# First norm's squares summed on TensorE, first layer's sine and cosine on GpSimd, two tiles of x on GpSimd's queue

## The chip, the cores and the metric

The kernel runs on one core of a Trainium2 chip. The metric is the device time of one launch in microseconds. The core has a matrix engine (TensorE, PE in the rows, its weight loads PEld), a vector engine (VectorE, DVE), a scalar engine (ScalarE, ACT), GpSimd (POOL) and a sync engine (SP) that here only issues transfers. Each engine works through its own list of instructions strictly in order, and an instruction that waits for another engine holds up everything behind it on its own engine.

## What is computed

Two transformer-like blocks over 512 tokens of width 1024, in f32. The change lies wholly within the start of the first layer of the first block:

```
h    = x * rsqrt(mean(x*x, axis=-1) + 1e-6) * norm_mix[0]
proj = h @ w_in[0]                 # q, k, v, conv inputs, u, gates
lam  = a_re + i*a_im;  dt = exp(log_dt)
lam_bar = exp(lam*dt) = exp(a_re*dt) * (cos(a_im*dt) + i*sin(a_im*dt))
b_bar   = (lam_bar - 1)/lam * b
states  = scan(lam_bar, u @ b_bar)    # the state-space branch, fed by u
```

After it come window attention, a short convolution, gates, a gated feed-forward part, a second such layer, then a block with two sparse attentions, an attention over a memory, and a feed-forward part.

## The kernel before

x lies transposed: eight tiles x0 to x7 of 128 features by 512 tokens, one f32 buffer each. A product is split for accuracy. `split` makes from a tile of x a rounded part (ScalarE, line 458) and a remainder (VectorE, line 462); `_split_` does the same with weights (lines 370 and 371). TensorE then does three matmuls for each pair of a 128x128 weight block and a tile: lines 438 to 440. The division by the norm is left until the products are evacuated: `RS` holds the inverse root, spread over all partitions.

Weights come in chunks of 512 KB, eight 128x128 blocks each, 24 matmuls for one chunk. There are three raw buffers, three rounded ones (`hi`) and three remainders (`lo`), used in turn, so chunk 6 needs the `hi` and `lo` of chunk 3 to be free. The first product, u, takes chunks 0 to 3: chunk 0 holds the blocks for x0 and x1, chunk 1 those for x2 and x3, and so on, four output tiles each, in four PSUM banks. Chunk 4 (the product k) reuses these banks, so it can't start before u is evacuated (line 580), which needs `RS`.

`RS` comes about as follows. `norm_add` (line 531) squares each tile on ScalarE and adds the squares into one tile `acc`, six of the seven additions on GpSimd (line 540). `norm_fin` sums `acc` over the partitions with 16 small matmuls against a column of ones (`tok_sums`, line 493 in `few`), takes the inverse root on VectorE (`rsqrt`, lines 482 to 488), and spreads it by four transposes (`nb`, line 504) and a copy on ScalarE (line 506).

Beside this `_ssm_tables` computes the tables of the state-space branch: a long run of tiny VectorE operations on 128x16 values (lines 837 to 849, 925 to 930): two exponentials, then `sincos`, then powers. `_gen_ssm` uses them.

The order of the instructions on each engine is made by a scheduler from priorities and its own estimates of durations. All transfers are issued by SP, in one order. A weight transfer waits in it until its raw buffer is free, and what stands behind it waits too.

Of the kernel before, what the change touches and what calls it, by code (L numbers as in the profile page):

```python
# [89 lines left out]
def _cst_layout():  # L90
    if _CST:
        return _CST
    o = 0
    for name, n in (("ident", 128), ("mask1", 256), ("maskc", 128), ("valid", 4), ("stack", 128),
                    ("ones2", 2), ("half2", 2), ("crope", 256)):
        _CST[name] = (o, n)
        o += n
    _CST["_n"] = (o, 0)
    return _CST
# [174 lines left out]
class _Net:  # L274
# [253 lines left out]
            self.nc.tensor.matmul(out[c:c + 64], pt[:, c:c + 64], v, start=start, stop=stop, skip_group_check=True)  # L528


    def norm_add(self, st, m, x, g, pool=False):
        nc = self.nc
        st["xg"][m] = self.split(x, g)
        if "acc" not in st:
            st["acc"] = self.slot()
            nc.scalar.activation(st["acc"], x, AF.Square)
        else:
            q = self.slot()
            nc.scalar.activation(q, x, AF.Square)
            (nc.gpsimd if pool else nc.vector).tensor_tensor(st["acc"], st["acc"], q, op=OP.add)  # L540
            self.rel(q)

    def norm_fin(self, st):

        st["rs"] = self.slot()
        yield
        ps = self.sb("nsum")
        self.tok_sums(lambda b: ps[:, b:b + 1], st["acc"])
        self.rel(st["acc"])
        r = self.small(4, tag="rs")  # L550
        self.rsqrt(r, ps[:, :4], 4, 1.0 / D, EPS)
        st["tok"] = r
        yield
        ps = self.sb("nb")
        self.bcast(lambda b: r[:, b:b + 1].to_broadcast([128, 128]), st["rs"], ps)
# [264 lines left out]
def _ssm_tables(N, i):  # L820

    nc = N.nc
    V = nc.vector
    W = 16
    n_tmp = [0]
    hold = [N.slot(), N.slot()]
# [7 lines left out]
    def ts(a, s1, s2=None, op0=OP.mult, op1=None, out=None, dt=FT):  # L834
        o = new(dt) if out is None else out
        if s2 is None:
            V.tensor_scalar(o, a, s1, None, op0=op0)
        else:
            V.tensor_scalar(o, a, s1, s2, op0=op0, op1=op1)
        return o  # L840

    def tt(a, b, op, out=None):
        o = new() if out is None else out
        V.tensor_tensor(o, a, b, op=op)
        return o

    def stt(a, s, b, op0, op1, out=None):
        o = new() if out is None else out
        V.scalar_tensor_tensor(o, a, s, b, op0=op0, op1=op1)
        return o  # L850

    def exp(x, out=None):
        x = ts(x, -87.0, 88.0, op0=OP.max, op1=OP.min)
        kf = ts(x, LOG2E, MAGIC, op0=OP.mult, op1=OP.add)
        ts(kf, MAGIC, op0=OP.subtract, out=kf)
        r = stt(kf, -0.693359375, x, OP.mult, OP.add)
        stt(kf, 2.12194440e-4, r, OP.mult, OP.add, out=r)
        p = ts(r, 1.0 / 5040.0)
        for k in (720.0, 120.0, 24.0, 6.0, 2.0, 1.0):
            stt(p, 1.0 / k, r, OP.add, OP.mult, out=p)  # L860
        ki = ts(kf, 127.0, op0=OP.add, dt=I32)
        k2 = ts(ki, 23, op0=OP.logical_shift_left, dt=I32)
        return stt(p, 1.0, k2.bitcast(FT), OP.add, OP.mult, out=out)
# [32 lines left out]
    lr, li = N.v(f"are{i}", 0, 16), N.v(f"aim{i}", 0, 16)  # L896
    dt = exp(N.v(f"ldt{i}", 0, 16))
    E = exp(tt(lr, dt, OP.mult))
    si, co = sincos(tt(li, dt, OP.mult))
    T = {}  # L900
    PWr = N.cp.tile([128, 16, 9], FT, tag="pwr", name="pwr")
    PWi = N.cp.tile([128, 16, 9], FT, tag="pwi", name="pwi")
# [81 lines left out]
    while n < 64:  # L984

        h = n // 2
        t1, t2 = t1s[:, :16].rearrange("p (a c) -> p a c", c=1), t2s[:, :16].rearrange("p (a c) -> p a c", c=1)
        hr, hi = Wr[:, :, h:h + 1], Wi[:, :, h:h + 1]
        cmul((Wr[:, :, n:n + 1], Wi[:, :, n:n + 1]), (hr, hi), (hr, hi), None, t1, t2)
        if n > 1:  # L990
            w1 = n - 1
            t1 = t1s[:, :16 * w1].rearrange("p (a c) -> p a c", a=16)
            t2 = t2s[:, :16 * w1].rearrange("p (a c) -> p a c", a=16)
            bb = lambda a: a[:, :, n:n + 1].to_broadcast([128, 16, w1])
            cmul((Wr[:, :, n + 1:2 * n], Wi[:, :, n + 1:2 * n]), (bb(Wr), bb(Wi)),
                 (Wr[:, :, 1:n], Wi[:, :, 1:n]), None, t1, t2)
        n *= 2
        yield
    N.rel(t1s, t2s, hold)
    T["w"] = (Wr, Wi)  # L1000
    N.ssm_t[i] = T
# [985 lines left out]
@with_exitstack  # L1987
def tile_two_blocks(ctx: ExitStack, tc: tile.TileContext, T, out, nch, parts=None, dump=None):
    nc = tc.nc
    N = _Net(ctx, tc, T, nch)  # L1990
    parts = parts or ("mix0", "ffn0", "mix1", "ffn1", "att2", "mem2", "mlp2")
    V, A = nc.vector, nc.scalar
    N.ssm_t = {}
    N.vec = N.keep([128, _vec_layout()["_n"][0]], FT, "vec")
    nk = _cst_layout()["_n"][0]
    N.cst = N.keep([128, -(-nk // 16) * 16], FT, "cst")[:, :nk]
    X = [N.slot() for _ in range(8)]
    nv = 64
    nc.sync.dma_start(N.vec[:, :nv], T["vec"][:, :nv])
    nc.sync.dma_start(X[0], T["xT"][0])  # L2000
    N.prefetch(1)
    for m in range(1, 8):
        nc.sync.dma_start(X[m], T["xT"][m])
        if m in (2, 5):
            N.prefetch(m)
        if m == 3:
            nc.sync.dma_start(N.vec[:, nv:], T["vec"][:, nv:])
    nc.sync.dma_start(N.cst, T["cst"])
    N.ident = N.c("ident")
    N.ones1 = N.c("ones2")[:, :1]  # L2010
    N.mask1 = N.keep([128, 256], BF, "mask1")

    wz = N.keep([128, 512], BF, "warm", "ssmc")
    nc.gpsimd.memset(wz, 0.0)
    ps = N.mm("warm")
    for _ in range(16):
        nc.tensor.matmul(ps, wz[:, :128], wz, start=True, stop=True)
    st = N.new_norm()

    def first(m):  # L2020
        nm = {"mix0": "norm_mix0", "ffn0": "norm_ffn0", "mix1": "norm_mix1", "ffn1": "norm_ffn1",
              "mem2": "norm2", "mlp2": "norm3"}.get(parts[0])
        if nm:
            N.norm_add(st, m, X[m], N.v(nm, m), pool=0 < m < 7)
        else:
            norm_add2(st, m, X[m], None)


    gg = N.keep([128, 16], FT, "gg")[:, :8]

    def norm_add2(st, m, x, _):
        st["xg"][m] = N.split(x, gg[:, m:m + 1])
        for key, g in (("acc", 1.0), ("acc2", N.v("norm_final", m))):
            if key not in st:
                st[key] = N.slot()
                A.activation(st[key], x, AF.Square, scale=g)
            else:
                q = N.slot()
                A.activation(q, x, AF.Square, scale=g)
                V.tensor_tensor(st[key], st[key], q, op=OP.add)  # L2040
                N.rel(q)

    for m in range(8):
        first(m)
        if m in (0, 2):
            N.presplit(m // 2 + 1)
    tab = None
    if parts[0] in ("mix0", "mix1"):
        tab = _ssm_tables(N, int(parts[0][3]))
        with tc.high_priority(offset=-600):  # L2050
            next(tab)
    V.tensor_tensor(gg, N.v("norm_final", 0, 8), N.v("norm1", 0, 8), op=OP.mult)
    V.tensor_copy(N.mask1, N.c("mask1"))
    for i in range(DEPTH):
        if f"mix{i}" in parts:
            st2 = N.new_norm()
            _gen_mix(N, i, X, st, st2, tab)
            tab = None
            st = st2
        if f"ffn{i}" in parts:  # L2060
            st2 = N.new_norm()
            if i + 1 < DEPTH and f"mix{i + 1}" in parts:
                N.side(_ssm_tables(N, i + 1))
            if i + 1 < DEPTH:
                _gen_ffn(N, i, X, st, st2, lambda m: N.v(f"norm_mix{i + 1}", m), N.norm_add)
                N.drain(*N.sides)
            else:
                _gen_ffn(N, i, X, st, st2, lambda m: None, norm_add2)
            st = st2
    if "att2" in parts:  # L2070
        st2 = N.new_norm()
        M = {}
        mem = _gen_memkv(N, M) if "mem2" in parts else None
        _gen_att2(N, X, st, st2, gg, mem)
        st = st2
    if "mem2" in parts:
        st2 = N.new_norm()
        if "att2" not in parts:
            M = {}
            for _ in _gen_memkv(N, M):  # L2080
                pass
        _gen_mem2(N, X, st, st2, M)
        st = st2
    if "mlp2" in parts:
        _gen_mlp2(N, X, st, out)
    else:
        for m in range(8):
            nc.sync.dma_start(out[m], X[m])
    tile_two_blocks.last = N
    assert N.wi == nch, (N.wi, nch)  # L2090
    return N.specs
# [26 lines left out]
```

## Time and profile before

| | us |
|---|---|
| median of 3 runs | 2381.6 (2377.18 to 2386.59) |
| the profiled execution | 2382.87 |
| its span, first to last instruction | 2381.1 |
| TensorE busy | 2346.6 (99%) |
| VectorE busy | 1440.0 (60%) |
| ScalarE busy | 854.7 (36%) |
| GpSimd busy | 28.4 (1%) |
| mean granted TensorE clock | 0.981 of full speed |

The shares are averages over the span. In a row of the timeline stand the start, the duration, the engine, the line, the operation, the tiles written and read with their shape, a count where equal rows were merged, and in brackets how long the engine had idled and what released it. A merged row's duration runs from the first start to the last end.

### The profile page before, as it was taken

How to read it: one execution, taken by the hardware profiler on the slowest of the kernel's cores; microseconds unless marked ns; L12 is line 12 of the kernel's file. 1: busy time of each engine (PE TensorE's matmuls, PEld its weight loads, DVE VectorE, ACT ScalarE, POOL GpSimd, SP SyncE). 2: the span in 40 equal slices, each digit the busy share in tenths (PEclk: the TensorE clock that was granted, in tenths of full speed). 3: DMA queues.
4: the chain of work that ended last, by engine and by line, in shares of the span. 5: the costliest groups of instructions: out<-in, count | busy, mean ns of one | idle time of the engine just before them, and what ended most of it. 6: DMA issues, size and time to landing. Idle time of an engine off the chain costs nothing. (4 is left out here: it accounts for less than half of the span.)

```text
span 2381.1 us, 33544 instructions
## 1 busy us (share of the span) xinstructions
PE 2346.6 (99%) x13197; PEld 1878.9 (79%) x13197; DVE 1440.0 (60%) x3038; ACT 854.7 (36%) x1442; POOL 28.4 (1%) x49
## 2 busy tenths in 40 slices
PE   8999999999999999999999999999899999999999
PEld 6777888888888887788888888887666677888887
DVE  9986567643435678755554343468879666543443
ACT  3243333432323323433333232244456445422322
POOL 1000000000000000000000000000000000000000
PEclk9999999999999999999999999999879799999999
DMA  5333332223332333333223333242202121332222
GB/s 193 99 91 93 116 102 98 97 93 99 101 99 96 117 109 90 91 104 102 96 97 98 98 98 106 98 148 90 74 2 72 36 71 54 98 97 97 95 95 86
DMA packets 96781, 225.97 MB, mean 95 GB/s; under 512 B 35440, under 2 KB 39664, under 8 KB 96624
## 3 DMA queue, kind: packets, MB, share of 16 engines
q1 hardware_dynamic: 96624, 223.84, 29.8%
q8 instruction: 104, 1.70, 0.3%
q14 instruction: 53, 0.43, 0.1%
HBM read 214.88 MB, written 8.91 MB: 94 GB/s over the span
## 5 line engine op out<-in xcount | busy, mean ns | idle before, releaser
L438 PE MATMUL mm<-r,hi 128*128 128x512 f32 x2928 | 1145.8, 391 | 3.0 <-DVE f L580 2.1
L440 PE MATMUL mm<-r,lo 128*128 128x512 f32 x2928 | 1139.0, 389 | 4.6 <-DVE lo L371 4.6
L439 PE MATMUL mm<-r,hi 128*128 128x512 f32 x2928 | 1139.1, 389 | 0.0
L370 ACT ACTIVATE hi<-raw 128x1024 fp32r<-128x1024 f32 (+1 forms) x374 | 395.6, 1058 | 1181.5 <-PE mm L439 828.6
L438 PEld LDWEIGHTS mm<-r,hi 128*128 128x128 f32 x2928 | 550.4, 188 | 130.3 <-issue 6.9
L440 PEld LDWEIGHTS mm<-r,lo 128*128 128x128 f32 x2928 | 550.3, 188 | 118.3 <-DVE lo L371 5.1
L439 PEld LDWEIGHTS mm<-r,hi 128*128 128x128 f32 x2928 | 550.4, 188 | 111.2 <-issue 0.6
L371 DVE TENSOR_TENSOR lo<-raw,hi 128x1024 fp32r<-128x1024 f32 (+1 forms) x374 | 455.6, 1218 | 214.5 <-ACT hi L370 211.6
L1154 DVE TENSOR_TENSOR f<-mm,f 128x512 f32<-128x512 f32 x88 | 60.8, 691 | 221.2 <-PE mm L440 221.2
L664 DVE TENSOR_TENSOR f<-mm,f 128x512 f32<-128x512 f32 x48 | 33.1, 689 | 94.7 <-PE mm L440 91.3
L458 ACT ACTIVATE r<-f 128x512 fp32r<-128x512 f32 x108 | 68.1, 631 | 59.0 <-DVE f L1160 29.1
L460 DVE TENSOR_TENSOR r<-f,r 128x512 fp32r<-128x512 f32 x108 | 74.0, 688 | 8.7 <-ACT r L458 6.5
L1176 DVE TENSOR_TENSOR f<-mm,f 128x512 f32<-128x512 f32 x48 | 32.8, 690 | 61.3 <-PE mm L440 61.3
L1965 DVE SCALAR_TENSOR_TENSOR f<-mm,f 128x512 f32<-128x512 f32 x32 | 22.1, 691 | 76.5 <-PE mm L440 76.5
L1587 PE MATMUL sc<-f,f 64*128 64x256 f32 (+3 forms) x192 | 61.8, 580 | 1.5 <-DVE sm L1624 1.5
L1629 ACT ACTIVATE f<-f,sm 128x128 f32<-128x128 f32 (+3 forms) x96 | 53.2, 556 | 21.9 <-DVE sm L1624 21.7
L1980 DVE TENSOR_TENSOR f<-mm,f 128x512 f32<-128x512 f32 x32 | 22.0, 691 | 61.6 <-PE mm L440 61.6
L1595 PEld LDWEIGHTS pt<-cst,f 128*128 128x128 f32 x240 | 28.8, 154 | 31.1 <-ACT f L1629 10.2
L1595 PE MATMUL pt<-cst,f 128*128 128x128 f32 x240 | 50.4, 324 | 2.5 <-ACT f L1629 2.3
L528 PEld LDWEIGHTS ot<-f,f 128*64 128x64 f32 x960 | 39.2, 152 | 17.1 <-issue 10.9
L528 PE MATMUL ot<-f,f 128*64 128x64 f32 x960 | 49.6, 247 | 0.2
L1600 ACT ACTIVATE f<-pt 128x128 f32<-128x128 f32 (+3 forms) x80 | 33.3, 433 | 44.7 <-PE pt L1595 44.6
(382 smaller groups left out, 1722.6 us busy)
## 6 DMA issues: line engine op xcount, KB each, us to landing
raw<-in_wp_dram SPq DMA_DIRECT2D x372, 512.0 KB, 3.5
f<-in_xT_dram SPq DMA_DIRECT2D x8, 256.0 KB, 5.1
ud<-f SPq DMA_DIRECT2D x8, 256.0 KB, 2.7
f<-ud SPq DMA_DIRECT2D x64, 32.0 KB, 3.3
f<-ud SPq DMA_DIRECT2D x8, 256.0 KB, 3.9
yd<-f SPq DMA_DIRECT2D x64, 32.0 KB, 3.0
f<-yd SPq DMA_DIRECT2D x8, 256.0 KB, 3.3
xd<-f SPq DMA_DIRECT2D x8, 256.0 KB, 2.3
```

The source lines that it names most:

```text
L370: self.nc.scalar.activation(h[:, s], r[:, s], AF.Copy)
L371: self.nc.vector.tensor_tensor(lo[:, s], r[:, s], h.bitcast(FT)[:, s], op=OP.subtract)
L438: nc.tensor.matmul(p, wh, rh, start=first, stop=False)
L439: nc.tensor.matmul(p, wh, rl, start=False, stop=False)
L440: nc.tensor.matmul(p, wl, rh, start=False, stop=last)
L458: nc.scalar.activation(h, src, AF.Copy, scale=1.0 if g is None else g)
L460: nc.vector.tensor_tensor(l, src, h.bitcast(FT), op=OP.subtract)
L528: self.nc.tensor.matmul(out[c:c + 64], pt[:, c:c + 64], v, start=start, stop=stop, skip_group_check=True)
L1154: V.tensor_tensor(z, ps, RS, op=OP.mult)
L1587: PE.matmul(ps[h][:, :w], q[t][hs, n * 128:(n + 1) * 128], k_of[br][hs, :w], start=True, stop=True)
L1595: PE.transpose(pt[:, b * 128:(b + 1) * 128], p[:, b * 128:(b + 1) * 128], N.ident)
L1629: A.activation(p[:, :w], p[:, :w], AF.Exp, bias=f[:, h:h + 1], scale=-1.0, accum_out=den[n, br][:, j:j + 1])
```

## The change

Three things are edited.

- The first norm no longer goes through `acc`. `norm_first` only splits a tile and remembers it. `norm_fin` squares all eight tiles and sums each over the partitions at once by 16 small matmuls that accumulate in PSUM: 128 in place of 16, two tiles after each of the first chunks.
- `sincos` of layer 0 is issued on GpSimd. [...] The code around it (`exp`, powers) stays on VectorE.
- x6 and x7 are issued from GpSimd's queue rather than from SP's, and the column of ones comes in an early transfer of its own.

```diff
-            (nc.gpsimd if pool else nc.vector).tensor_tensor(st["acc"], st["acc"], q, op=OP.add)
+            nc.vector.tensor_tensor(st["acc"], st["acc"], q, op=OP.add)
...
+    def norm_first(self, st, m, x, g):
+        st["xg"][m] = self.split(x, g)
+        st.setdefault("x", []).append(x)
...
-        self.tok_sums(lambda b: ps[:, b:b + 1], st["acc"])
-        self.rel(st["acc"])
+        if "x" in st:
+            for m, x in enumerate(st["x"]):
+                q = self.slot()
+                self.nc.scalar.activation(q, x, AF.Square)
+                for b in range(4):
+                    self.few(ps[:, b:b + 1], q[:, b * 128:(b + 1) * 128], self.ones1, start=(m == 0 and b == 0),
+                             stop=(m == 7))
+                self.rel(q)
+                if m % 2 and m < 7:
+                    yield
...
     def stt(a, s, b, op0, op1, out=None):
         o = new() if out is None else out
-        V.scalar_tensor_tensor(o, a, s, b, op0=op0, op1=op1)
+        if eng[0] is V:
+            V.scalar_tensor_tensor(o, a, s, b, op0=op0, op1=op1)
+        else:
+            z = ts(a, s, op0=op0, out=hold[1][:, 496:512])
+            tt(z, b, op1, out=o)
...
+    eng[0] = nc.gpsimd if i == 0 else V
     si, co = sincos(tt(li, dt, OP.mult))
+    eng[0] = V
...
-        nc.sync.dma_start(X[m], T["xT"][m])
+        (nc.sync if m < 6 else nc.gpsimd).dma_start(X[m], T["xT"][m])
...
-            N.norm_add(st, m, X[m], N.v(nm, m), pool=0 < m < 7)
+            N.norm_first(st, m, X[m], N.v(nm, m))
```

The scheduler makes a new order from this. ScalarE begins as follows in the changed program (f0 to f7 are x0 to x7, r their rounded parts, `DMASW` a transfer of GpSimd's queue, `DMAHW` one of SP's):

```order
L458 ACT_TABLE_LOAD [waits DMAHW0_49]
L458 ACTIVATE r12_124<-f6_78,vec_144 128x512 [waits DMASW0_49]
L458 ACTIVATE r0_112<-f0_72,vec_144 128x512 [waits DMAHW1_49]
L370 ACTIVATE hi_188<-raw_148 128x512 [waits DMAHW2_49]
L370 ACTIVATE hi_188<-raw_148 128x512 [waits DMAHW3_49]
L458 ACTIVATE r2_114<-f1_73,vec_144 128x512 [waits DMAHW4_49]
```

x6, which came nineteenth on ScalarE before, is the first tile that it takes, ahead of x0 and of the first weights.

VectorE, before, around the remainder of chunk 2 (`lo_400`), the end of the exponentials and the start of the tail of `sincos`:

```order
L849 SCALAR_TENSOR_TENSOR f16_88<-f16_88 128x16
L844 TENSOR_TENSOR f17_89<-f16_88 128x16 [waits DVE_49]
L371 TENSOR_TENSOR lo_400<-raw_159,hi_399 128x1024 [waits DMAHW3_49,Activation_49]
L844 TENSOR_TENSOR f17_89<-f17_89 128x16 [waits DVE_49]
L849 SCALAR_TENSOR_TENSOR f16_88<-f16_88 128x16 x2
L844 TENSOR_TENSOR r8_488<-f17_89 128x16 [waits DVE_49]
```

VectorE in the changed program, at the same place:

```order
L868 SCALAR_TENSOR_TENSOR f8_80<-f8_80 128x16 [waits DVE_49]
L862 TENSOR_TENSOR f9_81<-f8_80 128x16 [waits Pool_49] x2
L868 SCALAR_TENSOR_TENSOR f9_81<-f8_80 128x16
L868 SCALAR_TENSOR_TENSOR f8_80<-f8_80 128x16 [waits DVE_49]
L862 TENSOR_TENSOR f9_81<-f9_81 128x16 [waits DVE_49] x2
L371 TENSOR_TENSOR lo_400<-raw_160,hi_399 128x1024 [waits DMAHW4_49,Activation_49]
```

The squares of the cosine and the sine now wait for GpSimd (`Pool`), and the remainder of chunk 2 stands six instructions behind that wait.

GpSimd, in the changed program, from its start:

```order
L2030 DMA f6_78<-in_xT_dram 128x512
L2030 DMA f7_79<-in_xT_dram 128x512
L2042 MEMSET warm_166 128x512
L980 MEMSET bbz_473 128x512
L980 MEMSET bbz_477 128x512
L862 ISA
L862 TENSOR_TENSOR f8_80<-vec_144,f8_80 128x16 [waits DMAHW0_49,DVE_49]
L857 TENSOR_SCALAR f8_80<-f8_80 128x16 [waits Pool_49]
L855 TENSOR_SCALAR f8_80<-f8_80 128x16 [waits Pool_49]
L855 TENSOR_SCALAR f9_81<-f8_80 128x16 [waits Pool_49]
```

Two transfers stand ahead of the memset that the warming-up matmuls read, and 47 tiny instructions follow from the first of line 862 on, nearly each waiting for the one ahead of it. The product of the angle (`a_im*dt`) is the first of them. The six additions of line 540 are gone.

On TensorE the small matmuls of line 493 stand two tiles at a time: x0 and x1 after chunk 0, x2 and x3 after chunk 1, x4 to x7 after chunk 2. The four transposes `nb` come after all of chunk 3 (before, nine matmuls of chunk 3 stood behind them), then eight transposes of the state-space branch (`bl`), then chunk 4. On VectorE the last steps of `rsqrt` stand behind the remainders of chunks 2 to 6 and behind six 128x512 products of the state-space branch, which before came after the evacuation of u.

## Rows read from the trace of the kernel before

**Rows 1.** Three stretches: length, busy time (count) by engine, clock, DMA share, GB/s.

```profile
0.00:43.00 43.00, 33.92 (x159) 24.05 (x160) 39.04 (x167) 18.39 (x26) 10.49 (x14) 0.92 0.64 208
18.50:22.40 3.90, 3.90 (x11) 2.97 (x10) 3.90 (x19) 0.06 (x1) 0.00 (x0) 0.50 0.82 265
43.00:100.00 57.00, 54.99 (x290) 44.31 (x289) 56.84 (x136) 11.39 (x13) 1.64 (x4) 1.00 0.36 114
```

**Rows 2.** TensorE's waits in the first 80 us: total, times, longest.

```profile
PE mm L440 <- DVE lo L371: 4.6, 1, 4.6
PE mm L438 <- DVE f L580: 2.1, 1, 2.1
```

**Rows 3.** Timeline of TensorE and ScalarE in the first 41 us.

```profile
7.09 0.50 PE L438 MATMUL mm<-r,hi 128*128 128x512 f32 x1 [0.17 <-ACT hi L370]
...
22.64 0.39 PE L439 MATMUL mm<-r,hi 128*128 128x512 f32 x1
...
29.69 0.39 PE L440 MATMUL mm<-r,lo 128*128 128x512 f32 x1
30.01 0.43 PE L493 MATMUL nsum<-cst,f 128*32 128x1 f32 x32
30.37 0.50 PE L438 MATMUL mm<-r,hi 128*128 128x512 f32 x1
...
36.06 0.65 PE L504 MATMUL nb<-cst,rs 128*128 128x128 f32 x4 [0.86 <-DVE rs L488]
...
36.75 0.60 ACT L506 ACTIVATE f<-nb 128x512 f32<-128x512 f32 x1 [4.55 <-PE nb L504]
...
37.94 0.40 PE L440 MATMUL mm<-r,lo 128*128 128x512 f32 x1
40.43 0.50 PE L438 MATMUL mm<-r,hi 128*128 128x512 f32 x1 [2.09 <-DVE f L580]
```

**Rows 4.** Timeline of SP: three weight transfers, with x6 and x7 behind.

```profile
6.97 11.29 SPq L358 DMA_DIRECT2D raw<-in_wp_dram  x3
```

**Rows 5.** Timeline of VectorE, one row for each kind of work.

```profile
5.52 0.26 DVE L844 TENSOR_TENSOR f<-vec,f 128x16 f32<-128x16 f32 x2
...
16.69 1.21 DVE L371 TENSOR_TENSOR lo<-raw,hi 128x1024 fp32r<-128x1024 f32 x1
17.82 1.40 DVE L462 SCALAR_TENSOR_TENSOR r<-f,vec,r 128x512 fp32r<-128x512 f32 x2
...
30.09 0.16 DVE L837 TENSOR_SCALAR f<-pwr 128x16 f32<-128x16 f32 x1
...
31.13 0.28 DVE L2053 CAST mask<-cst 128x256 bf16<-128x256 f32 x1
...
35.86 0.14 DVE L488 SCALAR_TENSOR_TENSOR rs<-rt,ry 128x4 f32<-128x4 f32 x1
...
36.07 0.40 DVE L927 TENSOR_TENSOR bbr<-f,f 128x256 f32<-128x256 f32 x1
...
39.31 1.06 DVE L580 TENSOR_TENSOR f<-mm,f 128x512 f32<-128x512 f32 x1
```

**Rows 6.** Timeline of GpSimd, and two VectorE rows that met one of its additions.

```profile
0.24 0.10 POOL L2106 MEMSET const-float32-0.0<- 128x1 f32 x1 [0.24 <-issue]
...
8.97 2.73 POOL L540 TENSOR_TENSOR f<-f,f 128x512 f32<-128x512 f32 x2 [6.79 <-ACT f L539]
...
26.22 1.23 DVE L371 TENSOR_TENSOR lo<-raw,hi 128x1024 fp32r<-128x1024 f32 x1 [1.15 <-ACT hi L370]
26.85 1.74 POOL L540 TENSOR_TENSOR f<-f,f 128x512 f32<-128x512 f32 x1 [10.12 <-ACT f L539]
27.36 1.78 DVE L462 SCALAR_TENSOR_TENSOR r<-f,vec,r 128x512 fp32r<-128x512 f32 x1
```

**Rows 7.** Line 540's instructions: least, median and greatest duration in ns, first and last start.

```profile
L540 POOL TENSOR_TENSOR f<-f,f x6: 1264/1324/1739, 9.0 to 26.8; 128x512 f32<-128x512 f32 x6
L540 POOLq MODIFY_POOL_CONFIG  x2: 11/11/11, 2.1 to 2.2; - x2
```

**Rows 8.** One of TensorE's two waits between 80 and 200 us (the other is equal).

```profile
PE k L1101 <- DVE f L1092: 1.0, 1, 1.0
```

More of the change, by code (lines that the diff above doesn't have):

```diff
@@ L528, in apply_v, with norm_add @@
             self.nc.tensor.matmul(out[c:c + 64], pt[:, c:c + 64], v, start=start, stop=stop, skip_group_check=True)
-    def norm_add(self, st, m, x, g, pool=False):
+    def norm_add(self, st, m, x, g):
         nc = self.nc
@@ L547, in norm_fin @@
         ps = self.sb("nsum")
-        self.tok_sums(lambda b: ps[:, b:b + 1], st["acc"])
-        self.rel(st["acc"])
+        if "x" in st:
[9 more added lines that the diff above has]
+        else:
+            self.tok_sums(lambda b: ps[:, b:b + 1], st["acc"])
+            self.rel(st["acc"])
         r = self.small(4, tag="rs")
@@ L823, in _ssm_tables @@
     V = nc.vector
+    eng = [V]
     W = 16
@@ L836, in ts @@
         if s2 is None:
-            V.tensor_scalar(o, a, s1, None, op0=op0)
+            eng[0].tensor_scalar(o, a, s1, None, op0=op0)
         else:
-            V.tensor_scalar(o, a, s1, s2, op0=op0, op1=op1)
+            eng[0].tensor_scalar(o, a, s1, s2, op0=op0, op1=op1)
         return o
@@ L843, in tt @@
         o = new() if out is None else out
-        V.tensor_tensor(o, a, b, op=op)
+        eng[0].tensor_tensor(o, a, b, op=op)
         return o
@@ L848, in stt @@
         o = new() if out is None else out
-        V.scalar_tensor_tensor(o, a, s, b, op0=op0, op1=op1)
+        if eng[0] is V:
+            V.scalar_tensor_tensor(o, a, s, b, op0=op0, op1=op1)
+        else:
+            z = ts(a, s, op0=op0, out=hold[1][:, 496:512])
+            tt(z, b, op1, out=o)
         return o
@@ L998, in _ssm_tables @@
         yield
+    assert n_tmp[0] < 63
     N.rel(t1s, t2s, hold)
@@ L1998, in tile_two_blocks @@
     nv = 64
+    nc1 = _cst_layout()["ones2"][0]
     nc.sync.dma_start(N.vec[:, :nv], T["vec"][:, :nv])
@@ L2006, in tile_two_blocks @@
         if m == 3:
+            nc.sync.dma_start(N.cst[:, nc1:], T["cst"][:, nc1:])
             nc.sync.dma_start(N.vec[:, nv:], T["vec"][:, nv:])
-    nc.sync.dma_start(N.cst, T["cst"])
+    nc.sync.dma_start(N.cst[:, :nc1], T["cst"][:, :nc1])
     N.ident = N.c("ident")
```

## The prediction, made before the changed kernel ran

> **What bounds the kernel now.** I read the busy shares first: TensorE is busy 99% of the span, so the change can only win where TensorE stands still or runs slowly. The table by stretches comes next [rows 1]: in the first 43 us TensorE is busy for 33.92 us, so it stands still for 9.1 us there, and VectorE is busy for 39.04 of 43. After 43 us TensorE is nearly full. TensorE's waits of the first 80 us name the two largest [rows 2]: 4.6 us for the remainder of a weight chunk, 2.1 us for the evacuation of u. Both end with VectorE. After the longer wait the granted clock is 0.50, the lower of the two levels, for 3.90 us [rows 1]: work of 1.95 us at the upper one. So all that could be won in this stretch is about 9.1 + 1.95 = 11 us, 0.46% of the time, if no instruction were added and nothing else came in the way.
>
> The timeline says why VectorE is late. x6 and x7 stand behind three weight transfers on SP that took 11.29 us [rows 4], which only delays their own splits. What matters more is that VectorE and GpSimd hold each other up: a GpSimd addition that met a VectorE subtraction took 1.74 us, not the median 1.32, and the next VectorE split 1.78 us instead of some 0.70 [rows 5 to 7]. Six additions of 1.26 to 1.74 us stood on GpSimd, and VectorE lost most of that.
>
> **The change part by part.** All is reckoned from one moment: the start of chunk 4, the first chunk that needs the evacuation of u. It is 40.43 us before [rows 3].
>
> *The wait of 4.6 us goes.* The six additions no longer block VectorE, and the remainder of chunk 1 stands ahead of most tiny work. It should be there about when chunk 0 ends. With it goes the slow stretch behind it. But TensorE isn't free to run to chunk 4: what it waits for next is worked out below.
>
> *The small matmuls.* 16 of them cost TensorE from 30.01 to 30.37, some 0.4 us with the change of operands [rows 3]. 128 cost 8 x 0.4 = 3.2 us, 2.8 more. Chunks 0 to 3 are 96 matmuls; 31 of them took from 22.64 to 29.69 [rows 3], 0.227 us each, together 21.8 us. From 7.1 us TensorE alone would end chunk 3 at 7.1 + 21.8 + 3.2 = 32.1. The warming matmuls now wait for a memset behind two transfers on GpSimd. No row shows what issuing one costs there; on SP the three issues of Rows 4 were mostly waiting and give no price either. I take 1 us each and 2 us for the start of TensorE, and show that neither matters while VectorE is later than 34.
>
> *x6 first.* ScalarE and VectorE now begin with x6 from GpSimd's queue. No row shows such a transfer; SP's of the same size are the nearest. An early landing costs nothing, a late one moves VectorE back. This only counts if GpSimd's chain (next) is early, since otherwise VectorE waits there anyway.
>
> *The chain on GpSimd.* 47 tiny instructions, nearly all dependent. It starts when dt is ready, where the two products stand at 5.52 us now [rows 5]. One instruction: the low bound is the memset of one element per partition, 0.10 us, the high one the addition of 512, 1.32 us [rows 6, 7]. The gap between two dependent ones is some 0.08: a pair took 2.73 us with 1.3 us for each [rows 6]. A straight line between the two sizes gives 0.14 us for 16 elements. An addition reads two inputs where a memset reads none, so I take 0.20, still near the row of one element. 47 x (0.20 + 0.08) = 13.2 us, so the chain would end at 5.5 + 13.2 = 18.7 by itself.
>
> *The lock between the two engines.* In that time VectorE runs eight splits of x, two half remainders of chunk 0 and the remainder of chunk 1, eleven instructions of 0.7 us or more. Each makes one instruction of the chain wait; the addition of 1.74 us lost some 0.5 against its fellows [rows 6, 7]. 11 x 0.5 = 5.5 us. The chain ends at G = about 24.5 us. With the ends of the price, 0.14 and 0.45 us (16 elements at a third of the addition, beyond which I see no reason), G is 21.3 and 36; at the full price of an addition, the bound of the row, it would be 71.
>
> *VectorE waits for it.* What stands ahead of the wait is about eight splits at 0.70, 2.4 us of remainders and 20 tiny ones, some 10 us, plus a start about 1 us late: VectorE gets there at about 16.5 us. So it waits from 16.5 to 24.5, and with it the remainder of chunk 2, which TensorE wants at about 20 to 22 us. A wait of 4 to 6 us on TensorE takes the place of the one of 4.6.
>
> *From G to chunk 4.* VectorE must do, up to the end of the inverse root: five remainders at 1.21 (6.05), six 128x512 products at 0.70 (4.2, priced by the pair of splits), six 128x256 products and four copies of that size at 0.40 less an overlap of 0.07 (3.3), six of 64 elements at 0.15 (0.9, between the two sizes), and 79 tiny ones at 0.087 (6.9: twelve of them start between 30.09 and 31.13) [rows 5]. That is 21 us. Then the transposes, ScalarE's copy and the first evacuation: 0.65 + 0.60 + 1.06 [rows 3, 5] and 0.3 us of passing on, 2.6 us; the tiny work between fits beside the first two. Chunk 4 starts at G + 23.6 = 48.1 us. TensorE alone (32 to 34 us, then the weight split of chunk 6, which needs chunk 3's buffers, 2.3 us, and the same 2.6) would be there at 37 to 39, so VectorE decides.
>
> *What is paid back.* Eight transposes of the state-space branch are now done before chunk 4 instead of after: by the four of 0.65 us, about 1.0 us. VectorE is ahead by the six products and some tables when chunk 4 starts, about 7 us of its work, so the two waits of 1.0 us at 80 to 100 us [rows 8] should go: 1.9 us. On the other side TensorE stands still for some 4 us or more before chunk 4, much as before the slow stretch of Rows 1, and I charge the same 1.95 us of slow clock.
>
> Sum: (G + 23.6) - 40.4 - 1.0 - 1.9 + 1.95 = G - 17.8 us. With G = 24.5 that is +6.7 us. The profiled execution took 2382.87 us, span 2381.1 and 1.8 around it; it would become 2389.6. It lies 1.3 us above the median of the runs, so the median should go from 2381.6 to about 2388.
>
> **A rule weighed.** The trace shows GpSimd's configuration change at 2.1 us, and the first addition at 8.97 us, 0.08 us after its input [rows 6, 7]. So whatever loading went on was done within 6.8 us, and this kernel hid it. In the change the same instruction stands right before the chain, behind two transfers, and dt is ready at 5.5.
> The Trainium skill, GPSIMD Engine Reference, section 2.1 (Instruction dispatch), says that the first call to a freshly loaded kernel also pays a load of about 6 us that no instruction in the profile shows. By that rule the chain would begin near 10.5 us; no run here shows it yet.
> As a rival from rows: a start at up to 4.3 + 6.8 = 11.1 us, a chain of 13.2, five large VectorE instructions left to meet it (2.5): G = 26.8, +9.0 us, 2390.6.
>
> **The rivals.**
> *The chain is quick* (faster by a little). If a tiny instruction costs 0.10 with its gap, the chain ends before VectorE arrives, at 16.5 us. Then chunk 4 starts at 40.1, TensorE has no long stop, so no slow clock: 40.1 - 40.4 - 1.0 - 1.9 = -3.2 us, 2378. For it: the memset row, and VectorE's own 0.087. Against it: 47 dependent instructions, the gap of 0.08 alone is 3.8 us, and the lock.
> *The transfers of x6 and x7 are late.* They stand first on ScalarE and VectorE. If x6 came at 12 instead of 5 us, VectorE would arrive at 23.5 instead of 16.5, still no later than G; it takes away the gain of the quick chain, +4 us at the most (2385).
> The Trainium skill, SBUF — State Buffer, section "SBUF: two separate sides", warns of this: a transfer from GpSimd's queue gets its descriptors from GpSimd's cores, and VectorE instructions that hold the shared port keep them from writing (it gives 620 against 3100 ns). By it x6 would be some 2.5 us late, an estimate from that page's two figures; no run here shows such a transfer yet.
> *The chain is slow* (slower by over 0.5%). One mechanism, a tiny GpSimd instruction of 0.35 us or more with its gap of 0.08: G = 5.5 + 47 x 0.43 + 5.5 = 31.2, +13.4 us, 2395; at 0.45 it is +18, 2400. It decides from G = 29.7 on, where the sum passes 11.9 us. For it: the addition of 512 has far more than its share of elements can explain if its fixed part is large; one size doesn't tell. Against it: the memset of one element takes 0.10.
> *The change doesn't do what it says*: x6 and x7 come early, but nothing waited for them before the wait of 4.6 us; that part is worth nothing by itself.
>
> **How the numbers follow.** Forecast (G from 20 to 29): 0.45. Late start: 0.13. Quick chain or late transfers: 0.22. Slow chain: 0.20. About 0.5% (11.9 us) is what a measurement of this kernel can tell from no change. All but the slow chain lie within it; I add 0.02 for the upper edge of the forecast and 0.03 for a gain that I don't see: faster 0.03, same 0.75, slower 0.22. The range goes from the quick chain with 3 us more won (2375) to the chain at 0.45 us and a little on top (2402).
>
> **What would show it.** Right: VectorE idle for some 8 us before line 862's squares, released by GpSimd; tiny GpSimd rows of about 0.2 us; TensorE waiting some 5 us for the remainder of chunk 2 and again before the transposes `nb`; chunk 4 near 48 us; no wait for line 371 in chunk 1. Wrong: VectorE passing the squares without idling, or chunk 4 before 41 us (quick chain); GpSimd's first tiny row near 10 us (late start); ScalarE's first split after 7 us (late transfers); tiny rows of 0.35 us or more (slow chain).

## The result

The changed kernel takes 2392.2 us (median of 20 runs, 2375.84 to 2403.81), the kernel before 2371.53 us in the same series (20 runs, 2357.05 to 2386.59). The ratio is 1.0089, with a 95% interval of 1.0068 to 1.011: about 21 us slower. The forecast was +6.7 us. 2392.2 us lies within the range; the size of the loss was three times the one forecast.

Single executions of one kernel differ by 15 us and more. The kept profiles, one execution of each kernel, point far from the change: against the kernel before, none moves by more than 0.5 us between 400 and 1700 us, and by 1930 us they have moved by -16 to +3 us, with granted clocks of 0.81 to 0.91 there. So I also compare the profiles by *lag*: how much later than in the kernel before the same instruction starts. Two places serve: the first evacuation of u in layer 0 (line 580 of before, 39.31 us [rows 5]), and the last evacuation of u in the second layer (same line, 827.0 us before). In the changed kernel the lags are 8.2 and 16.9 us.

### The profile page after: what moved, and what is told of

Its sections match the earlier page's. It is cut to its first block, busy times and chain, and to the rows that moved or that the text cites. A ratio compares the mean times of both kernels' runs of the same rounds, so it can differ in the third digit from the quotient of the medians.

```text
span 2401.3 us, 34000 instructions
## 1 busy us (share of the span) xinstructions
PE 2361.3 (98%) x13421; PEld 1886.4 (79%) x13421; DVE 1433.3 (60%) x3003; ACT 855.2 (36%) x1442; POOL 36.7 (2%) x92
```

## The profile after

First the chain on GpSimd in the changed kernel's timeline (start, duration, engine, line, operation; line 862 was 844, 857 was 839, 855 was 837):

```profile
1.26 1.28 POOL L2030 DMA_DIRECT2D f<-in_xT_dram  x2 [0.81 <-POOLq L2134]
...
2.99 1.01 POOL L980 MEMSET bbz<- 128x512 f32 x2
6.63 0.22 POOL L862 TENSOR_TENSOR f<-vec,f 128x16 f32<-128x16 f32 x1 [2.63 <-DVE f L868]
...
11.79 1.35 POOL L857 TENSOR_SCALAR f<-f 128x16 f32<-128x16 f32 x1
...
16.70 0.25 POOL L855 TENSOR_SCALAR f<-f 128x16 f32<-128x16 f32 x1
17.04 0.22 POOL L862 TENSOR_TENSOR f<-f,f 128x16 f32<-128x16 f32 x1
...
23.54 0.76 POOL L862 TENSOR_TENSOR f<-f 128x16 f32<-128x16 f32 x4
```

The chain runs from 6.63 to 24.30 us. Where VectorE is idle, an instruction takes 0.20 to 0.26 us; from one start to the next it is 0.31 to 0.34 us where each needs the one ahead of it, and some 0.18 in the last ones, which mostly don't. Where it meets a large VectorE instruction, one takes up to 1.35 us.

VectorE's and ScalarE's timeline of the same kernel:

```profile
16.23 0.17 DVE L868 SCALAR_TENSOR_TENSOR f<-f 128x16 f32<-128x16 f32 x1
24.15 0.35 DVE L862 TENSOR_TENSOR f<-f 128x16 f32<-128x16 f32 x2 [7.75 <-POOL f L862]
...
44.18 1.22 DVE L371 TENSOR_TENSOR lo<-raw,hi 128x1024 fp32r<-128x1024 f32 x1
45.51 0.16 DVE L488 SCALAR_TENSOR_TENSOR rs<-rt,ry 128x4 f32<-128x4 f32 x1
47.50 1.08 DVE L596 TENSOR_TENSOR f<-mm,f 128x512 f32<-128x512 f32 x1 [0.20 <-ACT f L506]
```

```profile
5.41 1.33 ACT L458 ACTIVATE r<-f,vec 128x512 fp32r<-128x512 f32 x2 [1.53 <-DMA f<-in_xT_dram]
```

VectorE stands idle for 7.75 us, released by GpSimd; the inverse root is done at 45.51 and the first evacuation of u starts at 47.50 (39.31 before). x6 is there at 5.41 us. TensorE's waits of the first 60 us, which answer to [rows 2]:

```profile
PE nb L504 <- DVE rs L488: 6.1, 1, 6.1
PE mm L440 <- DVE lo L371: 3.5, 1, 3.5
PE warm L2045 <- POOL warm L2042: 3.1, 1, 3.1
```

The wait of 4.6 us for chunk 1's remainder is gone; 3.5 us for chunk 2's and 6.1 us for the inverse root stand in its place, and chunk 4 starts at 48.64 us (40.43 before [rows 3]).

So far the prediction's picture. Then the lag of the products goes between 5 and 11 us, as other work comes between them earlier or later than before, and is 9.1 us at the one that starts at 200 us in before. At 205 us it jumps to 18.5, and from 300 us on it stays at 16.8 to 16.9 until 1700 us. TensorE's timeline there, in the changed kernel:

```profile
209.04 0.33 PE L808 MATMUL pt<-cst,f 128*128 128x128 f32 x1
209.12 0.48 PE L440 MATMUL mm<-r,lo 128*128 128x512 f32 x1
209.53 1.13 PE L768 MATMUL s<-f,f 64*128 64x256 f32 x6
210.59 0.33 PE L808 MATMUL pt<-cst,f 128*128 128x128 f32 x1
210.85 0.70 PE L768 MATMUL s<-f,f 64*128 64x256 f32 x2
213.64 1.79 PE L808 MATMUL pt<-cst,f 128*128 128x128 f32 x6 [2.09 <-DVE f L796]
215.58 1.11 PE L808 MATMUL pt<-cst,f 128*128 128x128 f32 x4 [0.16 <-ACT f L810]
216.63 1.97 PE L816 MATMUL ot<-f,f 128*64 128x512 f32 x2
218.53 1.12 PE L808 MATMUL pt<-cst,f 128*128 128x128 f32 x4
219.57 1.35 PE L816 MATMUL ot<-f,f 128*64 128x512 f32 x4
220.85 0.50 PE L438 MATMUL mm<-r,hi 128*128 128x512 f32 x1
```

Scores (`s`), transposes of the probabilities (`pt`) and products with the values (`ot`) follow each other without products (`mm`) between them, from 209.53 to 220.85 us. The transposes wait 2.09 us for the division of the probabilities (line 796) on VectorE. VectorE was not idle:

```profile
207.51 1.23 DVE L1095 TENSOR_TENSOR_SCAN f<-f,f 128x512 f32<-128x512 f32 x1
208.66 0.33 DVE L796 TENSOR_SCALAR f<-f,dn 128x256 f32<-128x256 f32 x1
208.90 0.68 DVE L1097 TENSOR_TENSOR f<-f,wr 128x512 f32<-128x512 f32 x1
209.50 0.68 DVE L1098 TENSOR_TENSOR f<-f,wi 128x512 f32<-128x512 f32 x1
210.10 0.34 DVE L796 TENSOR_SCALAR f<-f,dn 128x256 f32<-128x256 f32 x1
210.37 1.22 DVE L371 TENSOR_TENSOR lo<-raw,hi 128x1024 fp32r<-128x1024 f32 x1
211.50 1.70 DVE L1106 TENSOR_TENSOR f<-f,f 64x252 f32<-64x252 f32 x4
213.23 1.67 DVE L796 TENSOR_SCALAR f<-f,dn 128x256 f32<-128x256 f32 x6
```

The scan of the state-space branch (lines 1095 to 1106) stood ahead of six of the eight divisions. The table by stretches (stretch, length, then busy time and count of PE, PEld, DVE, ACT, POOL; granted clock, DMA share, GB/s) has the price:

```profile
210.00:214.00 4.00, 1.91 (x11) 0.95 (x7) 3.93 (x10) 0.24 (x1) 0.00 (x0) 0.92 0.41 106
214.00:218.00 4.00, 3.84 (x12) 1.80 (x11) 3.93 (x24) 2.39 (x5) 0.00 (x0) 0.50 0.34 99
218.00:222.00 4.00, 4.00 (x13) 1.69 (x13) 0.00 (x0) 3.24 (x12) 0.00 (x0) 0.73 0.19 65
```

TensorE is idle for 2.1 of 4 us, and behind that the clock is at the lower level (0.50 is 1.2 GHz). The 29 matmuls of the attention from 209.53 to 220.85 us take 11.3 us; at the pace of their like in the kernel before (eight scores in 1.06 us, eight transposes in 0.97, four products with the values in 1.01) they would take 4.4, an estimate. So some 7 us are lost here; where the rest of the jump arises isn't shown. In the kernel before the attention stands between products there, and the row of 200 to 228 us has 27.57 us busy at clock 1.00:

```profile
200.00:228.00 28.00, 27.57 (x169) 20.27 (x168) 22.71 (x55) 11.59 (x25) 0.00 (x0) 1.00 0.28 86
```

## The experiments

Twelve kernels ran, each with 12 timed executions beside the kernel before. All lags are of the profiled execution, one for each kernel, so how far a lag differs from one execution to the next isn't known.

| kernel | first evacuation of u | lag there | lag at 827 us | ratio, 95% interval |
|---|---|---|---|---|
| the change | 47.5 | +8.2 | +16.9 | 1.0089 [1.0068, 1.011] |
| 1. sine back on VectorE | 40.9 | +1.6 | +10.0 | 1.0063 [1.0038, 1.0088] |
| 2. sine on GpSimd alone | 46.8 | +7.5 | +7.3 | 0.9989 [0.9955, 1.0023] |
| 3. sums on TensorE alone | 42.3 | +3.0 | +16.2 | 1.006 [1.0032, 1.0088] |
| 4. x6 and x7 alone | 39.5 | +0.2 | +1.3 | 0.9991 [0.9971, 1.0011] |
| 5. before, two more steps | 39.7 | +0.4 | +10.9 | 1.0047 [1.0021, 1.0073] |
| 6. changed, two steps held | 47.7 | +8.4 | +6.9 | 1.0017 [0.9984, 1.0051] |
| 7. changed, no stops | 43.0 | +3.7 | +4.4 | 1.002 [0.9991, 1.005] |
| 8. as 7, sine on VectorE | 34.3 | -5.0 | -1.6 | 1.0005 [0.9981, 1.003] |
| 9. as 7, powers later | 42.4 | +3.1 | -0.5 | 0.9974 [0.9944, 1.0003] |
| 10. as 8, powers later | 34.1 | -5.2 | -2.5 | 0.9974 [0.9952, 0.9997] |
| 11. as 9, readers behind the root | 37.0 | -2.3 | -4.6 | 0.9959 [0.9925, 0.9993] |
| 12. as 11, sine on VectorE | 35.2 | -4.1 | -1.6 | 0.9978 [0.9948, 1.0007] |

**Which part of the change costs?** Where no other kernel is named, an edit is against the changed kernel. Three theories: A, VectorE's wait for GpSimd's chain is the loss; B, with the sums on TensorE the inverse root stands behind other VectorE work; C, half of the loss is the order that the scheduler draws later on.

*1, sine back on VectorE.*
```diff
-    eng[0] = nc.gpsimd if i == 0 else V
+    eng[0] = V
```


> The change with the sine and cosine of layer 0 back on VectorE; sums on TensorE and x6, x7 on GpSimd's queue stay. Theory A (VectorE's wait for GpSimd's chain is the loss: 7.75 us idle, chunk 4 at 48.6 instead of 40.4): the idle goes, some 45 tiny instructions of 0.09 us come back (4 us), chunk 4 starts at 42 to 44 us and the time is 2370 to 2377, at most 0.2% above before. Theory B (the sums on TensorE are the loss, because the inverse root now stands behind the remainder of chunk 6, which needs chunk 3 to be done): chunk 4 stays at 46 us or later and the time at 2385 or more. Theory C (half of the loss, the 8.7 us around 205 to 225 us, is a matter of the order that the scheduler draws for attention and the state-space branch and has nothing to do with the start): chunk 4 as in A, but TensorE again has a wait of 2 us with a slow clock behind it between 100 and 300 us, or some other loss there, and the time depends on that.

The first evacuation is 6.6 us earlier than in the change, so the chain on GpSimd cost that much. The jump near 210 us stays (a lag of +3 before it, +10 after it), with the same wait: `pt` waits 2.1 us for the division.

*2, sine on GpSimd alone* (sums and x6, x7 as before).
```diff
-            N.norm_first(st, m, X[m], N.v(nm, m))
+            N.norm_add(st, m, X[m], N.v(nm, m), pool=0 < m < 7)
...
-        (nc.sync if m < 6 else nc.gpsimd).dma_start(X[m], T["xT"][m])
+        nc.sync.dma_start(X[m], T["xT"][m])
```


> The kernel before with one part of the change alone: sine and cosine of layer 0 on GpSimd. The squares are added on GpSimd and VectorE as before, x6 and x7 come from SP. Theory A: GpSimd has the 47 tiny instructions and six additions, VectorE waits for it before the remainder of chunk 2, and chunk 4 starts 4 to 8 us later than before (44 to 48 us): 2376 to 2382. Theory B: the inverse root stands before chunk 6's remainder as before, so chunk 4 starts within 2 us of before and the time is 2368 to 2375. Theory C: whichever start, a loss between 100 and 300 us may come on top.

The profile shows +7.5 us at the first place and the same to the end: no jump. TensorE waits 12.2 us for remainders. The ratio doesn't show these 7 us; its interval ends at 1.0023, just under the 1.003 that they come to, so the two views don't agree well and I rest nothing on the ratio of this one.

*3, sums on TensorE alone.*
```diff
-    eng[0] = nc.gpsimd if i == 0 else V
+    eng[0] = V
...
-        (nc.sync if m < 6 else nc.gpsimd).dma_start(X[m], T["xT"][m])
+        nc.sync.dma_start(X[m], T["xT"][m])
```


> The kernel before with one part alone: the first norm's squares summed on TensorE, with the column of ones in an early transfer. Sine and cosine on VectorE, x6 and x7 from SP. Theory A: no wait for GpSimd, no additions there that block VectorE; the wait of 4.6 us for chunk 1 goes and chunk 4 starts at 38 to 43 us: 2366 to 2375. Theory B: the inverse root waits for chunk 6's remainder, chunk 4 starts at 43 us or later, some 5 us or more slower than before. Theory C: a loss or a gain between 100 and 300 us comes on top of either.

Two thirds of the change's loss by the ratio, without GpSimd: +3.0 us at the first place and +16.2 later, with the same 2.1 us wait and jump.

*4, x6 and x7 on GpSimd's queue alone*, against the kernel before.
```diff
-        nc.sync.dma_start(X[m], T["xT"][m])
+        (nc.sync if m < 6 else nc.gpsimd).dma_start(X[m], T["xT"][m])
```


> The kernel before with one part alone: x6 and x7 on GpSimd's queue. Theories A and B: nothing waited for these two tiles before the wait of 4.6 us, so the start changes by less than 2 us either way (the warming matmuls begin 1.8 us later, TensorE's first product with them, as in the changed kernel's 9.4 us): 2367 to 2375. In this order the inverse root stands ahead of the remainders of chunks 5 and 6, so the wait of 2.1 us before chunk 4 may go too (down to 2365). Theory C: a loss or gain between 100 and 300 us comes on top.

Worth nothing by itself, as the prediction's last rival had it.

A is some 40% of it, then (6.9 of 16.9 us go with the sine back on VectorE), and the jump comes with the sums. What in the sums? `norm_fin` is now a chain of five steps in place of two: it stops three times between the squares. The loop that drains it steps every side generator along with it, so the tables of the state-space branch get two more steps before chunk 4, and the state-space work starts two chunks earlier against the attention. That is theory D.

*5, the kernel before with the two steps and nothing else.*
```diff
     N.drain(fin)
+    if i == 0:
+        N.tick()
+        N.tick()
```


> The kernel before, with two more steps of the side work (tables and state space) ahead of chunk 4, as the three stops in the summing of squares give them in the changed kernel; nothing else is changed. Theory D (the two steps shift the state-space work against the attention, so that scores, transposes and values of a block meet without products between them some 205 to 225 us into the span): chunk 4 within 2 us of before, a wait of about 2 us of TensorE for the division of the probabilities with a granted clock near 0.5 behind it, some 8 us lost there, ratio to before 1.0035 (1.002 to 1.005). Theory A (only VectorE's wait for GpSimd costs time) and theory B (only the place of the inverse root): no such wait, ratio 1.000.

The start is as before (+0.4 us), then the clump and the jump appear. TensorE's timeline of this kernel (line 795 is the transposes, 783 the division), without any product from 206 to 215 us:

```profile
203.77 0.70 PE L755 MATMUL s<-f,f 64*128 64x256 f32 x4
206.11 0.33 PE L795 MATMUL pt<-cst,f 128*128 128x128 f32 x1 [1.64 <-DVE f L783]
208.11 1.78 PE L795 MATMUL pt<-cst,f 128*128 128x128 f32 x6 [1.67 <-DVE f L783]
210.05 1.11 PE L795 MATMUL pt<-cst,f 128*128 128x128 f32 x4 [0.16 <-ACT f L797]
```

and its row by stretches, 24.30 us busy at clock 0.88 where before had 27.57 at 1.00:

```profile
200.00:228.00 28.00, 24.30 (x120) 15.55 (x120) 18.86 (x65) 9.96 (x27) 0.00 (x0) 0.88 0.23 66
```

Ratio 1.0047, as D has it: no sum moved, no sine moved, and some 10 us lost. Here TensorE waits for the division twice, 1.64 and 1.67 us.

*6, the changed kernel whole, with the state-space work of layer 0 held back two steps.*
```diff
+    if i == 0:
+        yield
+        yield
     T = N.ssm_t.pop(i)
```


> The changed kernel whole, but the state-space work of the first layer starts two steps later, so that it stands to the attention as before. Theory D: chunk 4 late by about 8 us as in the changed kernel, no wait of 2 us for the division of the probabilities near 210 us, the lag stays 8 to 9 us to the end; ratio to before 1.0035 to 1.004, where the changed kernel has 1.009. Theories A and B: what is lost after 200 us comes from the late start, so it stays; ratio 1.007 to 1.009.

The same start as the change (+8.4), and no jump: the lag falls to 6.9 us, where D had 8 to 9. The waits of 60 to 300 us shrink to three short ones, 1.2 us together, and the row of 200 to 228 us is nearly full again:

```profile
PE pt L808 <- DVE f L796: 1.2, 3, 0.5
```

```profile
200.00:228.00 28.00, 27.54 (x163) 20.07 (x160) 22.52 (x57) 10.38 (x24) 1.08 (x2) 1.00 0.27 84
```

5 and 6 settle it: two steps of a side generator, let in by where the sums stop, are worth some 10 us a long way from the place edited. The times agree: the interval of 5 lies above 1, and those of 6 and of the change don't meet.

*7, the changed kernel without the three stops.*
```diff
-                if m % 2 and m < 7:
-                    yield
```


> The changed kernel without the three stops in the summing of squares, so that no further step of the side work is let in; sums on TensorE and the sine on GpSimd stay. VectorE's work ahead of the inverse root shrinks by about 13 us by the durations of the rows. Theory D: no clump near 210 us, and chunk 4 within 3 us of before, bounded by the end of GpSimd's chain at 24 us and the rest of VectorE's work (24 + 14 = 38 us); ratio 0.998 to 1.002. Theory A: the wait for GpSimd's chain stays, chunk 4 late by 5 us or more, ratio 1.002 to 1.004. Theory B: the inverse root stands ahead of the remainder of chunk 6 and its loss goes, ratio as by D.

No jump, as D says, but the first evacuation is 3.7 us late and chunk 4 4.3 us (44.71): VectorE still idles 8.3 us for GpSimd, then TensorE 4.7 us for the inverse root. For chunk 4 D had at most 3 us and A at least 5, so both miss.

*8, as 7, with the sine on VectorE.*
```diff
-    eng[0] = nc.gpsimd if i == 0 else V
+    eng[0] = V
```


> Sums of the squares on TensorE and the last tiles of x on GpSimd's queue as in the changed kernel, but the sine back on VectorE and no stops in the summing. VectorE's work ahead of the inverse root is some 19 us by the durations of the rows, so TensorE decides alone: chunk 4 at 36 to 39 us, 1.5 to 4.5 us ahead of before. Theory D: no clump near 210 us, and the gain stays to the end, ratio 0.998 to 0.9995. Theory B: the same. Theory A: as D, since nothing waits for GpSimd. If the sums on TensorE themselves cost time (3.2 us of small matmuls in the stretch), ratio 1.000 to 1.001.

The inverse root is done at 23.99 us and TensorE waits for it no more: first evacuation 5.0 us ahead. Against experiment 1, which differs by the stops alone, that is 6.6 us: B was right in this, that the side work let in stood ahead of the inverse root. Of the gain 3.4 us are given back in two places. By 100 us it is 1.3 us: TensorE waits 1.8 us for `k` and the clock of 80 to 90 us is 0.83, while the kernel before loses its own 2.0 us there. Near 153 us it is another 1.8 us, and that wait is again for the division, behind a scan:

```profile
152.93 0.33 PE L806 MATMUL pt<-cst,f 128*128 128x128 f32 x1 [1.57 <-DVE f L794]
```

```profile
150.00:160.00 10.00, 8.43 (x42) 5.67 (x41) 9.70 (x27) 3.60 (x8) 0.00 (x0) 1.00 0.23 71
```

Here three products stand behind each of the first transposes, the clock stays at 1.00, and the wait costs little more than its own length. Whether the products around it made it cheaper than the wait of 2 us at 210 us, or its being shorter, isn't shown.

**Wait or lock?** The sine on GpSimd costs 8.7 us at the first place (7 against 8). Either VectorE's wait does it or the lock between the two engines.

*9, as 7, with the first powers one step later.*
```diff
     eng[0] = V
+    if i == 0:
+        yield
     T = {}
```


> The changed kernel without the three stops, and with the first powers of the poles, which read GpSimd's sine and cosine, moved one step of the side work later, behind the inverse root; the sine stays on GpSimd. Theory A (VectorE's wait for GpSimd's chain, not the lock between the engines, made the sine on GpSimd cost 7 to 9 us at chunk 4): VectorE no longer waits ahead of the inverse root, the wait of 4.7 us of TensorE for it goes, first evacuation of u at 34 to 36 us (43.0 without the move, 34.3 with the sine on VectorE), and the lag at 800 us is -6 to -2 us; ratio 0.997 to 1.000. Its rival (the lock: every chain instruction delays a large VectorE instruction): the first evacuation stays at 40 to 43 us, lag +1 to +4; ratio 1.000 to 1.002.

The edit didn't take the wait away. VectorE's waits show it still there:

```profile
DVE f L860 <- POOL f L860: 8.0, 1, 8.0
```

It was aimed at the wrong readers. What VectorE waits with is the squares for the doubled angles, not the powers, and they stood there already in the changed kernel (the row at 24.15 us) and in 7:

```profile
24.24 0.35 DVE L860 TENSOR_TENSOR f<-f 128x16 f32<-128x16 f32 x2 [8.33 <-POOL f L860]
```

The edit moves them one step later in the program too, and the scheduler put them back into the same place. So the 42.4 us say nothing on wait or lock. That the lag falls to -0.5 us later goes with the missing waits for `k`: before has two of 1.0 us, here there is none. The other 1.6 us of the fall aren't explained.

*10, as 9, but the sine on VectorE, and GpSimd's memset for the warming matmuls first.*
```diff
-    eng[0] = nc.gpsimd if i == 0 else V
...
     X = [N.slot() for _ in range(8)]
+    wz = N.keep([128, 512], BF, "warm", "ssmc")
+    nc.gpsimd.memset(wz, 0.0)
...
-    wz = N.keep([128, 512], BF, "warm", "ssmc")
-    nc.gpsimd.memset(wz, 0.0)
```


> Sums on TensorE, sine on VectorE, no stops, first powers one step later, and GpSimd's memset for the warming matmuls ahead of its two transfers. Here nothing waits for GpSimd, so by theory A and by the lock alike: first evacuation of u at 33 to 35 us, warming matmuls 1.5 to 2 us earlier. The state-space work is one step behind that of the kernel without stops, and 24 products stand ahead of the first eight matmuls k: the wait of 1.8 us there and its slow clock (3.3 us together) should go. Lag at 800 us -3 to -6 us, ratio 0.9975 to 0.999; by theory D no wait above 1 us at 200 to 228 us.

The start as expected; the wait for `k` did not go (2.2 us), so half of the gain is lost again by 100 us (the clock of 43 to 100 us is 0.94). That expectation failed.

*11, as 9, with all readers of sine and cosine behind the inverse root*, by a factor of one made from it.
```diff
-        st["tok"] = r
+        st["tok"] = self.tok = r
...
     if i == 0:
         yield
+        one = new()[:, :1]
+        V.tensor_scalar(one, N.tok[:, :1], 0.0, 1.0, op0=OP.mult, op1=OP.add)
+        ts(si, one, out=si)
+        ts(co, one, out=co)
```


> As the kernel with the first powers one step later (sine on GpSimd, no stops), but GpSimd's sine and cosine are multiplied by one before they are read, and that one is made from the inverse root (root times 0 plus 1), so that no reader of them can stand ahead of the inverse root on VectorE. Theory A: VectorE doesn't idle for 8 us at 16 us, TensorE's wait of 4.6 us for the inverse root goes, first evacuation of u at 33 to 36 us, lag at 800 us -9 to -5 us (the kernel with the powers later had -0.5 with 42.4 us), ratio 0.996 to 0.998. The lock: VectorE's large instructions of 16 to 24 us each lose about 0.5 us to the chain and the first evacuation comes at 37 to 41 us; lag -4 to -1, ratio 0.998 to 1.000.

VectorE's timeline, now without the long wait:

```profile
17.27 1.22 DVE L371 TENSOR_TENSOR lo<-raw,hi 128x1024 fp32r<-128x1024 f32 x1
...
18.72 1.27 DVE L371 TENSOR_TENSOR lo<-raw,hi 128x1024 fp32r<-128x1024 f32 x1
...
22.53 0.16 DVE L482 TENSOR_SCALAR ra<-nsum 128x4 f32<-128x4 f32 x1 [1.73 <-PE nsum L493]
...
24.70 0.16 DVE L488 SCALAR_TENSOR_TENSOR rs<-rt,ry 128x4 f32<-128x4 f32 x1
...
26.43 0.37 DVE L853 TENSOR_SCALAR f<-f,f 128x16 f32<-128x16 f32 x2 [1.37 <-POOL f L860]
```

and GpSimd beside it:

```profile
17.34 1.26 POOL L853 TENSOR_SCALAR f<-f 128x16 f32<-128x16 f32 x1
18.69 0.22 POOL L860 TENSOR_TENSOR f<-f,f 128x16 f32<-128x16 f32 x1
19.00 1.10 POOL L853 TENSOR_SCALAR f<-f 128x16 f32<-128x16 f32 x1
```

The inverse root comes at 24.70 us in place of 31.37 (9). VectorE's remainders take 1.22 and 1.27 us, their usual time, while GpSimd's instructions of 0.25 us take 1.26 and 1.10: the lock was paid by the chain, not by VectorE. So it was the wait. The expected figures alone don't decide it: the first evacuation came at 37.0, 1 us later than A had it and at the lock's edge, as two products of 0.68 us stand ahead of it, and the lag of -4.6 us lies between the two ranges. The rows decide: the idle time of 8 us is gone and no remainder lost the 0.5 us that the lock would cost. The ratio of 0.9959 is the lowest of the study and its interval lies below 1; it overlaps with those of several others.

*12, the same with the sine on VectorE.*
```diff
-    eng[0] = nc.gpsimd if i == 0 else V
```


> As the kernel whose readers of sine and cosine stand behind the inverse root, but with the sine back on VectorE; all else, the multiplication by one included, is the same. It prices the sine on GpSimd once VectorE doesn't wait for it. If the 4 us of tiny work that VectorE takes on were on the path: first evacuation of u at 39 to 41 us (37.0 with the sine on GpSimd), lag at 800 us -2 to 0 us. If that work lies in time in which VectorE waits for the sums anyway (1.7 us idle there before the inverse root): first evacuation at 34 to 38 us, lag -3 to -7 us, ratio 0.997 to 0.999; then the order alone made the kernel faster and GpSimd had no part in it.

The start is even earlier (35.2 us): the tiny work fits into time in which VectorE waits for the sums (2.59 us here). But the lag at 827 us is -1.6, not -4.6, and the expected -3 to -7 was missed. VectorE has that work more, and pays at 80 to 100 us, where TensorE waits for `k`:

```profile
PE k L1129 <- DVE f L1120: 2.8, 1, 2.8
```

With the sine on GpSimd (11) that wait is gone. GpSimd's part is worth 3.0 us by one profile of each; the ratios of 11 and 12 overlap, so the times don't show it.

## Why the prediction was right and wrong

- *The chain, G = 24.5 us* (its terms add up to 18.7 + 5.5 = 24.2). It ended at 24.30. The start was 6.63 in place of 5.5 (two memsets on GpSimd, 2.99 to 4.00 us, held up VectorE's exponential of dt). Up to 16.05 us, beside the eleven large VectorE instructions, 16 steps took 9.4 us; at the later pace (0.31 to 0.34, two of 0.19) they would have taken 4.9, so the lock cost some 4.5 us in place of 5.5. The other 31 took 8.2 us. The chain by itself was thus 4.9 + 8.2 = 13.1 us, and 13.2 was forecast, though not as 47 equal steps. That G came out within 0.2 us is in part luck: a start 1.1 us late and a lock 1.0 us cheaper cancel.
- *VectorE waits, some 8 us.* 7.75 us. Chunk 2's remainder was forecast 4 to 6 us late for TensorE and was 3.5.
- *Chunk 4 at 48.1 us.* 48.64. G + 23.6 held to 0.7 us.
- *The late start.* By the Trainium skill, GPSIMD Engine Reference, section 2.1, about 6 us of loading would come with the first call to a freshly loaded kernel. The trace doesn't show it: the first instruction started at 6.63 us, as soon as its input was there, 2.6 us after the configuration change on GpSimd (`MODIFY_POOL_CONFIG`, 3.9 to 4.0 us). *Late transfers:* x6 was there at 5.41 us; no delay is to be seen, but VectorE's first large instruction came at 6.69 us, so what that rival feared wasn't put to the test. *Slow chain, quick chain:* 0.31 us lies between their 0.43 and 0.10.
- *What is paid back: this step failed.* The prediction counted the eight transposes of the state-space branch that now come before chunk 4 as 1.0 us saved, and two waits of 1.0 us [rows 8] as gone. The early transposes were the sign that the side work had moved two steps ahead of the attention. That moved the scan in front of the division of the probabilities at 210 us, and the term that was put at -2.9 + 1.95 = -0.95 us was +8.7 us (16.9 - 8.2). One of the waits for `k` stayed, with 1.2 us. Experiment 6, without the two steps, gives the term nearly as forecast: 8.4 us at the first evacuation, 8.9 by 45 us, behind the slow clock (0.5 in place of 1.95), 6.9 with no wait for `k` left (2.0 in place of 1.9); only the 1.0 us for early transposes has no place in it.
- *The sum.* +16.9 us by the profile at 827 us; the profiled execution ended with +20.2, of which the rest arose after 1700 us. The interval of the ratio, 16 to 26 us, holds both.
- *Luck in the number.* The range went up to 2402 and was built on a median of 2381.6 us; in the series of the result the kernel before took 2371.53. The loss of 20.7 us on top of 2381.6 is 2402.3, just beyond the range. By the prediction's own line of 0.5% the result of 0.9% is slower; that had 0.22, nearly all for a slow chain, which didn't come.

So the forecast of the edited stretch was right within 1 us, and the forecast of the kernel was wrong because nothing behind 100 us was looked at; the signs that it named all lay in the first 50 us, and they came true. TensorE's order of instructions has `s`, `pt` and `ot` there without products between them; that could be read without any time.

## What to carry to other kernels

Where side work is stepped by a generator's stops, each stop added or removed is a change of the schedule for everything that runs beside it: count the steps before and after, and look through the whole order for runs of small matmuls without products between them. Work handed to a slow engine pays only if its first reader stands behind everything that is urgent on the fast engine; look in the trace which reader waits, and don't rely on its place in the program, since the scheduler may put it back (9); a data dependence held it (11). And an edit that frees the fast engine may pay far from its place (here 3 us by the profiles, at a wait between 80 and 100 us), so the lag is to be followed past the edit.

## What the runs showed of the hardware

- 128x16 f32 instructions on GpSimd take 0.20 to 0.26 us each; in a dependent run they start every 0.31 to 0.34 us, the independent ones at the end of the chain every 0.18. VectorE starts such small ones every 0.09 us where other work lies between those that depend on each other (28.30 to 28.64 us in experiment 9), and a dependent run every 0.21 (seven steps of the exponential, 5.12 to 6.58 us in the changed kernel). So in a dependent run GpSimd was some 1.5 times slower here.
- Where such a GpSimd instruction meets a VectorE remainder of 1.2 us, it takes up to 1.35 us (11.79 us in the changed kernel) and VectorE's time is unchanged (1.23 us there). By the Trainium skill, SBUF — State Buffer, section "SBUF: two separate sides", whichever starts first, a VectorE instruction with two inputs in SBUF or a GpSimd one that reads SBUF, gets the shared port pair for its whole length. These rows agree, and in them the engine with the short instructions pays. The other way round, two memsets of 128x512 on GpSimd (1.01 us together) stretched a VectorE instruction on 128x16 to 1.31 us.
- A wait of 2 us of TensorE with only the attention's matmuls around it cost far more than itself: the granted clock was 0.50 for the next 4 us and 0.73 for the 4 after that (the change, 214 to 222 us). A shorter one of 1.57 us with products around it left the clock at 1.00 (experiment 8, 150 to 160 us).
